# A list schedule that knows the array tile of each TensorE step and counts a change of tile

## The chip, the core and the metric

The kernel runs on one core of one Trainium2 chip. The core has TensorE (PE in the profile; its weight loads are PEld), VectorE (DVE), ScalarE (ACT), GpSimd (POOL) and SyncE (SP), which issues DMAs. Each engine executes its instructions in the order in which the program gives them and waits on semaphores for the others. The metric is the device time of one launch in microseconds (us). Three runs of the kernel before took 1405.84 to 1409.65 us, with a median of 1408.31 us.

## What is computed

One layer of a hybrid decoder: 16 meta tokens and 1024 tokens of width 1024, float32. Four mixers share one input projection, their outputs are concatenated and projected, and a mixture of 16 experts with two experts per token follows.

```python
h = layernorm(concat(meta, x))
ua, ub, uc, ud = split(h @ w_in)
ya = swa_attention(ua)          # window 128, 4 heads, softmax with sinks
yb = diff_attention(ub)         # two softmax maps per head, p0 - lam * p1
yc = rwkv7_mix(uc)              # the step below, token after token
yd = conv_module(ud)            # depthwise convolution of width 31, group norm, silu
h = layernorm(ALPHA * h + concat(ya, yb, yc, yd) @ w_out)
h = layernorm(ALPHA * h + moe(h))

def step(S, inp):               # rwkv7: 4 heads, state S of 64 x 64 per head
    r_t, w_t, k_t, v_t, kk_t, a_t = inp
    sa = einsum('bhij,bhj->bhi', S, -kk_t)
    S = S * w_t[:, :, None, :] + sa[..., None] * (kk_t * a_t)[:, :, None, :] + v_t[..., None] * k_t[:, :, None, :]
    return S, einsum('bhij,bhj->bhi', S, r_t)
```

## The kernel before

The program has three stretches. Stage 1 (up to about 206 us) normalizes the input and makes the projected columns of the RWKV mixer and of the convolution. Stage 2 makes the remaining projections, the convolution, both attentions and the RWKV mixer, and then the output projection with the routing. Stage 3 runs the experts. The change touches the order of stage 2 alone, up to the output projection.

**Stage 2's parts.** The projections (`project`, matmuls on L860) make ten column units, each from 72 matmuls: three column chunks (400, 384 and 256 wide), each in three steps of eight matmuls (high by high, high by low, low by high halves). Their results go out to DRAM and come back as the attention's operands once all of them are done (`switch`, then `load_qk` on L1302 and `values` on L1269). The convolution (`conv`) is 62 VectorE operations on 128 x 1024 (60 of them on L1184), followed by a group norm (`Norms`: a TensorE step on L1140, a subtraction, a square on ACT, a TensorE step on L1151, then logarithm and exponential on ACT). `swa` and `diff` are the attention blocks: scores (L1360, L1361, L1464), softmax, transposes (L1387, L1395, L1525), products with the values (L1407, L1408, L1539), and a last transpose of the outputs (L1585).

**The RWKV mixer** works on 17 chunks of 64 tokens in nine groups: the first has one chunk, the others two. `prep(i)` builds a group's matrices: gram matrices (L939), transposes (L966, L983), one product on L993, and then the inverse of a triangular matrix X in five levels. A level is a transpose on VectorE (L1010), a TensorE step (L993, `prep<-Tt,gs`), a masking on VectorE (L1017), a TensorE step (L993, `prep<-X,um`) and an addition on VectorE (L1024). A group's first X is made on GpSimd (L953, L954) and waits for the last X of the group before, so that the levels of all groups form one chain. `chain(i)` then takes the state through each chunk: L1056, a VectorE addition, L1079, copies on ACT and VectorE, L1095, VectorE for the new state (L1102), and L1118 and L1120 for the chunk's output. `rwkv_post` (norm, bonus, gate: L1140 to L1226) finishes each half of the sequence. The output projection (`out_block`, first matmul on L1823) needs all four mixers.

**What sets the order.** Each piece of work is a `Step` with an engine, a cost, dependencies and a priority. `Steps.run` simulates the engines and, again and again, takes the step that can start first; among steps that can start at the same time, the lower priority number wins. A step can start when its dependencies have ended (plus 0.2 where they ran on another engine), when its buffers are free and when its engine is free:

```python
t = max(t, free.get(s.eng, 0.0))
key = (t, s.prio, s.n)
```

The priorities of the projections are 20 to 29, of the attention blocks 10 to 57, of RWKV groups 0 to 3 just under 0, and of groups 4 to 8 between 10 and 55 (`PRG`). The code of the chosen step is written out at once, so the order of choice is the order on each engine.

**Tiles of the array.** Most TensorE steps use the whole array, 128 rows by 128 columns. The RWKV steps use part of it: 64 x 64 (L966, L993, L1056, L1079, L1118), 64 x 128 (L939, L983) or 128 x 64 (L1095, L1120). The profile prints this tile behind the names of a matmul (`128*128`, `64*64`).

## Time and profile before

| what | value |
|---|---|
| median of three runs | 1408.31 us (1405.84 to 1409.65) |
| the profiled execution's own time | 1411.35 us |
| its span, first to last instruction | 1409.5 us |
| mean granted TensorE clock, share of full speed | 0.927 |
| PE busy, share of the span | 1221.4 us, 87% |
| DVE / ACT / POOL busy | 908.9 / 627.2 / 278.5 us |
| stage 2 from the first projection to the first output projection matmul | 206.3 to 693.7 us |

A busy engine is one that has an instruction under way. On PE, consecutive matmuls overlap, and so the time that a matmul really takes from the engine is read from the distance between starts. A timeline row merges like instructions that follow one another; on PE one program matmul of float32 appears as two records in the rows of the RWKV steps.

### The profile page before, as it was taken

How to read it: one execution, taken by the hardware profiler on the slowest of the kernel's cores; microseconds unless marked ns; L12 is line 12 of the kernel's file. 1: busy time of each engine (PE TensorE's matmuls, PEld its weight loads, DVE VectorE, ACT ScalarE, POOL GpSimd, SP SyncE). 2: the span in 40 equal slices, each digit the busy share in tenths (PEclk: the TensorE clock that was granted, in tenths of full speed). 3: DMA queues.
4: the chain of work that ended last, by engine and by line, in shares of the span. 5: the costliest groups of instructions: out<-in, count | busy, mean ns of one | idle time of the engine just before them, and what ended most of it. 6: DMA issues, size and time to landing. Idle time of an engine off the chain costs nothing. (4 is left out here: it accounts for less than half of the span.)

```text
span 1409.5 us, 22368 instructions
## 1 busy us (share of the span) xinstructions
PE 1221.4 (87%) x8095; PEld 1006.0 (71%) x8095; DVE 908.9 (64%) x1682; ACT 627.2 (44%) x1109; POOL 278.5 (20%) x252
## 2 busy tenths in 40 slices
PE   5998899999979899789699948898989899889950
PEld 4886799887857788667477736776777777767840
DVE  7556739996235667477667785856457863866175
ACT  6453211233124655357733225656346653645151
POOL 3523203321111122133001121111111111121100
PEclk9999999999987999879899968998999999999985
DMA  8213245421180230501252547969887992996352
GB/s 205 84 47 111 103 132 183 140 86 56 54 213 20 55 88 11 113 24 57 85 179 91 179 151 232 357 191 302 239 240 233 326 341 65 333 317 196 97 181 120
DMA packets 165466, 219.65 MB, mean 156 GB/s; under 512 B 36047, under 2 KB 134491, under 8 KB 165037
## 3 DMA queue, kind: packets, MB, share of 16 engines
q1 hardware_dynamic: 156604, 188.66, 42.1%
q0 software_dynamic: 8688, 28.87, 8.6%
q8 instruction: 86, 1.41, 0.4%
q14 instruction: 88, 0.71, 0.2%
HBM read 174.38 MB, written 45.46 MB: 156 GB/s over the span
## 5 line engine op out<-in xcount | busy, mean ns | idle before, releaser
L454 PE MATMUL acc<-hh,wh 128*128 128x256 f32 (+2 forms) x288 | 96.8, 337 | 0.0
L454 PE MATMUL acc<-hh,wl 128*128 128x256 f32 (+2 forms) x288 | 93.3, 325 | 0.6 <-DVE wl L342 0.6
L1184 DVE SCALAR_TENSOR_TENSOR CY<-MX,cvw,CY 128x1024 f32<-128x1024 f32 x60 | 89.1, 1506 | 0.1
L2121 PE MATMUL rw<-wh,at 128*128 128x512 f32 x224 | 82.8, 420 | 7.2 <-ACT at L2096 3.1
L454 PE MATMUL acc<-hl,wh 128*128 128x256 f32 (+2 forms) x288 | 87.5, 322 | 0.0
L1665 DVE TENSOR_TENSOR wl<-MX,wh 128x1024 fp32r<-128x1024 f32 x66 | 78.2, 1219 | 6.8 <-ACT wh L1661 4.7
L2125 POOL DMA_INDIRECT acc__132<-y,ixs x21 | 40.8, 1945 | 181.5 <-issue 59.4
L1665 DVE TENSOR_TENSOR wol<-MX,woh 128x1024 fp32r<-128x1024 f32 x51 | 61.1, 1222 | 13.7 <-ACT woh L1661 12.5
L1661 ACT ACTIVATE wh<-MX 128x1024 fp32r<-128x1024 f32 x66 | 66.9, 1050 | 3.8 <-DMA MX<-in_exp_w_dram 2.2
L1482 ACT ACTIVATE E<-sc,nm 128x144 f32<-128x144 f32 (+7 forms) x64 | 48.0, 751 | 27.0 <-DVE nm L1476 22.6
L454 PEld LDWEIGHTS acc<-hh,wh 128*128 128x128 f32 x288 | 55.5, 193 | 5.7 <-issue 5.2
L1661 ACT ACTIVATE woh<-MX 128x1024 fp32r<-128x1024 f32 x51 | 52.1, 1051 | 13.5 <-DMA MX<-in_exp_w_dram 7.7
L2121 PEld LDWEIGHTS rw<-wh,at 128*128 128x128 f32 x224 | 43.7, 196 | 18.4 <-ACT at L2096 3.6
L454 PEld LDWEIGHTS acc<-hh,wl 128*128 128x128 f32 x288 | 55.3, 192 | 1.9 <-DVE wl L342 0.9
L1823 PE MATMUL oacc<-woh,mh 128*128 128x512 f32 x128 | 54.7, 428 | 1.7 <-ACT woh L1775 1.7
L2097 DVE TENSOR_TENSOR xte<-acc,xte 128x512 fp32r<-128x512 f32 x44 | 28.5, 684 | 38.8 <-ACT xte L2096 38.8
L454 PEld LDWEIGHTS acc<-hl,wh 128*128 128x128 f32 x288 | 53.3, 189 | 0.0
L1823 PE MATMUL oacc<-wol,mh 128*128 128x512 f32 x128 | 52.0, 406 | 1.5 <-DVE wol L1778 1.5
L1823 PE MATMUL oacc<-woh,ml 128*128 128x512 f32 x128 | 51.3, 401 | 0.0
L1506 POOL TENSOR_TENSOR E<-E,rho 128x272 f32<-128x272 f32 (+3 forms) x16 | 21.0, 1313 | 150.1 <-DVE rho L1500 71.2
L1539 PE MATMUL tp<-vs,at 128*128 128x128 f32 x352 | 48.8, 290 | 0.6 <-ACT at L1528 0.3
L2096 ACT ACTIVATE at<-tp 128x256 fp32r<-128x256 f32 x46 | 17.6, 382 | 70.8 <-PE tp L2094 56.4
(472 smaller groups left out, 3452.9 us busy)
## 6 DMA issues: line engine op xcount, KB each, us to landing
MX<-in_exp_w_dram SPq DMA_DIRECT2D x192, 256.0 KB
MX<-in_exp_w_dram SPq DMA_DIRECT2D x48, 512.0 KB
CY<-in_exp_w_dram SPq DMA_DIRECT2D x64, 256.0 KB
raw<-in_w_in_dram SPq DMA_DIRECT2D x20, 512.0 KB
qk<-dqk SPq DMA_DIRECT2D x64, 130.0 KB
CY<-in_exp_w_dram SPq DMA_DIRECT2D x16, 512.0 KB
dab<-ab SPq DMA_DIRECT2D x2, 2176.0 KB
qk<-dqk SPq DMA_DIRECT2D x16, 260.0 KB
```

Of the source, the lines that this page charges most:

```text
L454: T.matmul(v.acc[:, :wid], wt[:, k], x[:, k, c0:c0 + wid], start=(z + y == 0 and wt is w.h), stop=(z + y == len(ks) - 1))
L1184: V.scalar_tensor_tensor(y, hc[:, M + j:M + j + S], cvw[:, ct, j:j + 1], y, op0=ALU.mult, op1=ALU.add)
L1482: ACT.activation(w.E[:, c, off:W], w.sc[c][:, :W - off], AF.Exp, bias=w.nm[:, c:c + 1], scale=-1.0, accum_out=w.s[:, c:c + 1])
L1506: G.tensor_tensor(w.E[:, 1, :W], w.E[:, 1, :W], w.rho.to_broadcast([P, W]), op=ALU.mult)
L1539: T.matmul(o, w.at[:, j], vs[:, j, vc], start=(j == 0), stop=(j == blocks[-1]))
L1661: ACT.activation(slot_h[i % HLS][0], raw[i], AF.Copy)
L1665: eng.tensor_tensor(l, raw[i], h.bitcast(F32), op=ALU.subtract)
L1823: T.matmul(v.o, x_[:, k], y_[k][:, 512 * n:512 * n + 512], start=(i == 0 and j == 0), stop=False)
L2096: ACT.activation(dst[:, 0, s], tb[:, :m * P], AF.Copy)
L2097: V.tensor_tensor(dst[:, 1, s], tb[:, :m * P], dst[:, 0, s].bitcast(F32), op=ALU.subtract)
L2121: T.matmul(o[n], at[:, x, k * P:(k + 1) * P], w[k][y][:, n * 512:n * 512 + 512], start=(k == 0 and (x, y) == (0, 0)), stop=(k == 3 and x = ...
L2125: G.indirect_dma_start(out=acc_, out_offset=bass.IndirectOffsetOnAxis(ap=ix[:, 0:1], axis=0), in_=y, in_offset=None, compute_op=ALU.add)
```

## The change

Each TensorE step gets a `kind`, a pair of letters for its first and its last matmul's tile: `m` for the whole array (the default), `q` for 64 x 64, `r` for 64 x 128 and `c` for 128 x 64. The scheduler keeps the tile that the last TensorE step left behind. Where a step's first tile is another one, its earliest start on TensorE is counted 0.09 later. The step's cost is as before, no instruction's code is changed, and no priority.

```diff
-    LAT = LATN
+    LAT, CHANGE = LATN, 0.09
...
-    def add(self, eng, cost, fn, deps=(), prio=0.0, take=(), use=()):
+    def add(self, eng, cost, fn, deps=(), prio=0.0, take=(), use=(), kind=None):
+
         s = Step()
+        s.kind = kind or ("m", "m")
...
     def run(self):
-        free = {}
+        free, tile_ = {}, "m"
...
-                t = max(t, free.get(s.eng, 0.0))
+                t = max(t, free.get(s.eng, 0.0) + (self.CHANGE if s.eng == "PE" and s.kind[0] != tile_ else 0.0))
                 key = (t, s.prio, s.n)
...
             s.end = free[s.eng] = t + s.cost
+            if s.eng == "PE":
+                tile_ = s.kind[1]
             s.fn()
...
-        a = add("PE", .12 * n, vt1, [o.loaded], pr, take=[sv, o.sbz], use=[o.slot])
+        a = add("PE", .12 * n, vt1, [o.loaded], pr, take=[sv, o.sbz], use=[o.slot], kind="qq")
...
-            a = add("PE", .06 * n, b1, [vd], pr, take=[sb], use=[o.slot])
+            a = add("PE", .06 * n, b1, [vd], pr, take=[sb], use=[o.slot], kind="rr")
...
-                a = add("PE", .43, h1, sad, pr, take=[sh, ns], use=[o.sbz])
+                a = add("PE", .43, h1, sad, pr, take=[sh, ns], use=[o.sbz], kind="cc")
```

The other RWKV steps get their letters in the same way: `rr` for L939; `qq` for the steps on L993, L1056 and L1079; `cc` for the output of a chunk on L1118 and L1120.

The instructions of the projection stretch, the attention and the RWKV mixer come out in another order on every engine. Up to the first RWKV step of stage 2, and from the first matmul of the output projection on, TensorE's order is the same as before. In the changed kernel the line numbers are 4 or 5 higher.

**TensorE, where the first RWKV group began.** `acc` is a projection's accumulator, `wh` and `wl` its weights, `hh` and `hl` the input; `prep` is the RWKV preparation. Before:

```order
L860 MATMUL acc<-hh,wh_1755 128x384 x8
L860 MATMUL acc<-hh,wh_1755 128x256 x8
L860 MATMUL acc<-hl,wh_1755 128x384 x8
L939 MATMUL prep<-abv 128x128 x2
L860 MATMUL acc<-hh,wl_1756 128x384 x8
L939 MATMUL prep<-abv 128x128 x2
L860 MATMUL acc<-hl,wh_1755 128x256 x8
L860 MATMUL acc<-hh,wh_1866 128x400 x8
L966 MATMUL prep<-c__63,vch 64x64 x4
L860 MATMUL acc<-hh,wl_1756 128x256 x8
```

The same place in the changed kernel:

```order
L864 MATMUL acc<-hh,wh_1755 128x384 x8
L864 MATMUL acc<-hh,wh_1755 128x256 x8
L864 MATMUL acc<-hl,wh_1755 128x384 x8
L864 MATMUL acc<-hl,wh_1755 128x256 x8
L864 MATMUL acc<-hh,wl_1756 128x384 x8
L864 MATMUL acc<-hh,wl_1756 128x256 x8
L864 MATMUL acc<-hh,wh_1866 128x400 x8
L864 MATMUL acc<-hh,wh_1866 128x384 x8
```

The RWKV steps have left the projections: the first of them now stands behind the last projection matmul, and only the convolution's norm steps (L1145, L1156) stand between projections.

**TensorE, ahead of the output projection.** `E` holds softmax rows, `vs` and `at` values and transposed weights, `o` the attention's output, `chain` the RWKV chunks. Before:

```order
L1525 MATMUL tp<-c__63,E 128x128 x3
L1539 MATMUL tp<-vs,at 128x128 x6
L1525 MATMUL tp<-c__63,E 128x128 x4
L1539 MATMUL tp<-vs,at 128x128 x4
L1223 MATMUL tp<-xg,g2s 128x512 x2
L1585 MATMUL tp<-c__63,o 128x128 x4
L1823 MATMUL oacc<-woh_6941,mh_6953 128x512
```

The same place in the changed kernel; ahead of the first row stand eight more steps on L998 without another step between them, and behind the last one follow L1156, L1228 and the first output projection matmul (L1828):

```order
L998 MATMUL prep<-X,um 64x64 x8
L1084 MATMUL chain<-r,X 64x64 x4
L1100 MATMUL chain<-bz 64x64 x4
L1125 MATMUL chain<-gs,bz 64x64 x2
L1123 MATMUL chain<-abv,s_6744 64x64 x4
L1125 MATMUL chain<-gs,bz 64x64 x2
L1061 MATMUL chain<-s_6880,abv 64x64 x4
L1084 MATMUL chain<-r,X 64x64 x4
L1125 MATMUL chain<-gs,bz 64x64 x2
L1123 MATMUL chain<-abv,s_6880 64x64 x4
L1125 MATMUL chain<-gs,bz 64x64 x2
L1145 MATMUL tp<-MX,bdm 128x512 x2
```

What stood last before was the attention; what stands last now is the RWKV mixer's last two groups and its post-processing. Behind the last `tp<-vs,at` step there are 22 steps on L998 in the changed kernel (the two of each of ten levels, and one product for each of two groups) and none before.

## Rows read from the trace of the kernel before

**Rows 1.** Busy time by stretch (us from:to, length, engines with counts, PEclk, DMA, GB/s).

```profile
206.20:389.80 183.60, 179.81 (x1654) 154.94 (x1655) 132.41 (x188) 49.90 (x91) 46.96 (x34) 1.00 0.32 100
389.80:425.80 36.00, 25.44 (x316) 20.79 (x315) 10.63 (x31) 9.99 (x29) 3.13 (x6) 0.77 0.82 208
425.80:684.10 258.30, 231.12 (x2369) 193.64 (x2366) 171.93 (x545) 148.88 (x394) 62.49 (x60) 0.90 0.21 51
```

**Rows 2.** Timeline of TensorE in the projections (start, us, engine, line, names, tile, count).

```profile
212.06 3.01 PE L860 MATMUL acc<-hh,wl 128*128 128x400 f32 x16
214.91 2.55 PE L860 MATMUL acc<-hh,wh 128*128 128x256 f32 x16
217.30 2.56 PE L860 MATMUL acc<-hl,wh 128*128 128x256 f32 x16
...
222.09 2.50 PE L860 MATMUL acc<-hh,wh 128*128 128x384 f32 x16
224.42 1.57 PE L860 MATMUL acc<-hl,wh 128*128 128x384 f32 x8
...
348.70 2.66 PE L860 MATMUL acc<-hl,wh 128*128 128x256 f32 x16
351.29 0.68 PE L993 MATMUL prep<-Tt,gs 64*64 64x64 f32 x16
```

**Rows 3.** Groups of VectorE from 214.3 to 327.6 us (count, busy, mean ns, idle before).

```profile
L1184 DVE SCALAR_TENSOR_TENSOR CY<-MX,cvw,CY 128x1024 f32<-128x1024 f32 x55 | 83.1, 1526 | 0.1
L877 DVE SCALAR_TENSOR_TENSOR qlo<-acc,qhi 128x400 fp32r<-128x400 f32 (+2 forms) x18 | 9.0, 503 | 4.8 <-ACT qhi L873 4.8
```

**Rows 4.** The convolution's line: duration min/median/max in ns, first and last start.

```profile
L1184 DVE SCALAR_TENSOR_TENSOR CY<-MX,cvw,CY x60: 1232/1274/3250, 197.5 to 326.3; 128x1024 f32<-128x1024 f32 x60
```

**Rows 5.** Timeline of TensorE behind the projections: first value transposes, first differential scores.

```profile
405.27 1.94 PE L1282 MATMUL tp<-c__63,E 128*128 128x128 f32 x8 [5.40 <-DMA E<-dvv]
...
425.85 0.70 PE L1464 MATMUL sc<-qk,qk 128*128 128x144 f32 x2
```

**Rows 6.** Levels of the RWKV inverse: timeline of PE and DVE, clock of 423 to 426.

```profile
389.75 0.68 PE L993 MATMUL prep<-Tt,gs 64*64 64x64 f32 x16
390.95 0.68 PE L993 MATMUL prep<-X,um 64*64 64x64 f32 x16 [0.53 <-DVE um L1017]
391.68 0.42 DVE L1024 TENSOR_TENSOR X<-prep,X 128x256 f32<-128x256 f32 x1 [0.38 <-PE prep L993]
386.03 0.45 DVE L1010 STREAM_TRANSPOSE Tt<-X 128x256 f32<-128x256 f32 x1
...
423.00:426.00 3.00, 2.32 (x33) 2.02 (x33) 0.55 (x3) 0.00 (x0) 0.00 (x0) 0.50 0.00 0
423.15 1.12 PE L993 MATMUL prep<-Tt,gs 64*64 64x64 f32 x16 [0.78 <-DVE gs L942]
424.80 1.12 PE L993 MATMUL prep<-X,um 64*64 64x64 f32 x16 [0.53 <-DVE um L1017]
425.96 0.42 DVE L1024 TENSOR_TENSOR X<-prep,X 128x256 f32<-128x256 f32 x1 [1.22 <-PE prep L993]
```

**Rows 7.** Timeline: a group's first X, a conv norm, and stage 2's end.

```profile
310.16 2.52 POOL L953 TENSOR_TENSOR X<-gs,c 64x256 f32<-64x256 f32 x2
283.96 1.98 PE L1140 MATMUL tp<-CY,bdm 128*128 128x512 f32 x4
293.49 1.15 ACT L1168 ACTIVATE sq<-sq 128x512 f32<-128x512 f32 x2
...
662.75 0.34 PE L1120 MATMUL chain<-gs,bz 128*64 128x64 f32 x4
682.61 1.50 PE L1539 MATMUL tp<-vs,at 128*128 128x128 f32 x8
685.89 1.40 DVE L1226 SCALAR_TENSOR_TENSOR MX<-MX,lxb,tp 128x512 f32<-128x512 f32 x2
693.67 0.80 PE L1823 MATMUL oacc<-woh,mh 128*128 128x512 f32 x1 [1.72 <-ACT woh L1775]
```

More of the change, by code (lines that the diff above doesn't have):

```diff
@@ L942, in f2 @@
                 V.tensor_tensor(o.gs[:, par], small["pu"].rearrange("p (a c) -> p a c", c=P)[:, :n], b3(gmask, n), op=ALU.mult)
-            m = add("PE", .22 * n, f1, [o.loaded] + gfirst, pr, take=[sl] + ([] if gfirst else [o.sgs]), use=[o.slot] + ([o.sgs] if gfirst else []))
+            m = add("PE", .22 * n, f1, [o.loaded] + gfirst, pr, take=[sl] + ([] if gfirst else [o.sgs]), use=[o.slot] + ([o.sgs] if gfirst else []),
+                    kind="rr")
             gfirst = gfirst or [m]
@@ L1001, in lv2 @@
             ACT.activation(o.lv.rearrange("p a b c -> p (a b c)"), small["pu"][:, :n * C], AF.Copy)
-        a = add("PE", .12 * n, lv1, gdone + [vd], pr, take=[sl_, o.slv], use=[o.sgs, o.sbz])
+        a = add("PE", .12 * n, lv1, gdone + [vd], pr, take=[sl_, o.slv], use=[o.sgs, o.sbz], kind="qq")
         o.lvd = add("ACT", act(n * C), lv2, [a], pr, use=[sl_, o.slv])
@@ L1026, in prep @@
             a = add("DVE", dve(n * C), tr, [o.Xd], pr, take=[stt], use=[sX])
-            a = add("PE", .12 * n, u1, [a], pr, take=[su_, sum_], use=[stt, o.sgs])
+            a = add("PE", .12 * n, u1, [a], pr, take=[su_, sum_], use=[stt, o.sgs], kind="qq")
             a = add("DVE", dve(n * C), u2, [a], pr, use=[su_, sum_])
-            a = add("PE", .12 * n, x1, [a], pr, take=[sx_, sX1], use=[sum_, sX])
+            a = add("PE", .12 * n, x1, [a], pr, take=[sx_, sX1], use=[sum_, sX], kind="qq")
             o.Xd = add("DVE", dve(n * C), x2, [a], pr, use=[sx_, sX, sX1])
@@ L1064, in f3 @@
                         G.tensor_scalar(w.sp0[:, ct], w.s0[:, ct], pend[:, ct, c:c + 1], None, op0=ALU.mult)
-                a = add("PE", .25, f1, [sdone, o.loaded], pr, take=[ss_, sr], use=[sslot, o.slot])
+                a = add("PE", .25, f1, [sdone, o.loaded], pr, take=[ss_, sr], use=[sslot, o.slot], kind="qq")
                 rd = add("DVE", dve(P), f2, [a, o.lvd], pr, use=[ss_, sr, o.slv])
@@ L1085, in g3 @@
                 V.tensor_copy(o.bz[HALF[1], 1, 1, ci::o.nc], p2(small["cs"])[HALF[1]])
-            a = add("PE", .25, g1, [rd, o.Xd], pr, take=[scs], use=[sr, o.sX])
+            a = add("PE", .25, g1, [rd, o.Xd], pr, take=[scs], use=[sr, o.sX], kind="qq")
             sad = [add("ACT", act(P), g2, [a] + o.bzd, pr, use=[scs, o.sbz]), add("DVE", dve(P), g3, [a] + o.bzd, pr, use=[scs, o.sbz])]
@@ L1123, in y2 @@
                     ACT.activation(MX[:, 4:6, (c - 1) * C:c * C], p2(small["cy"]), AF.Copy)
-                a = add("PE", .7, y1, sad, pr + .05, take=[sy], use=[s0slot, o.slot, o.sbz, o.sgs])
+                a = add("PE", .7, y1, sad, pr + .05, take=[sy], use=[s0slot, o.slot, o.sbz, o.sgs], kind="cc")
                 ydone[c] = add("ACT", act(P), y2, [a], pr + .05, use=[sy])
```

## The prediction

> **What bounds the kernel now.** I read the stretches first, then TensorE's timeline in each, then the waits at their ends. From the first projection matmul to the last one, TensorE is busy in 179.8 of 183.6 us at full clock [rows 1]: it is the bound there, and what it does besides the 720 projection matmuls (RWKV groups 0 to 3, four norm steps, changes of tile) lengthens the stretch. VectorE is nearly as full, with the convolution until 327.6 us (its last tap starts at 326.3 and takes 1.27) [rows 4]. Then come 36 us in which TensorE is busy in 25.4 and the DMA engines in 82% of the time: the attention's operands come back from DRAM, and 5.40 us of that is a bare wait [rows 1, 5]. From 425.8 to 684.1 us attention and RWKV alternate; TensorE is busy in 231.1 of 258.3 us, so 27.2 us are idle. At 684.1 the last value product ends [rows 7], and 9.6 us later the output projection begins. Before the change, then, attention and RWKV end together.
>
> **What a change of tile costs.** Sixteen projection matmuls (eight of 256 and eight of 400 columns) take 217.30 - 214.91 = 2.39 us from start to start among their like, and 351.29 - 348.70 = 2.59 us with an RWKV step of another tile on either side [rows 2]. That is 0.10 us a side; the RWKV step pays something too. So the 0.09 that the scheduler now counts is the right size. Counting the changes in the two orders gives 356 before and 258 now in stage 2: 98 fewer, which is 98 x 0.10 = 10 us of TensorE's time.
>
> **What the change moves.** The saving is small beside the new order. The projections are always ready and of the default tile; an RWKV step is of another tile and so counts as startable 0.09 later; and the start time is compared ahead of the priority. So whole-array steps win over RWKV steps for as long as one is ready, whatever the priorities say, and RWKV goes to where nothing else can start. By the order, nothing of RWKV stands among the projections any more, and the work is pushed back towards the end. With it go its issues on the queues: on SP most of the group loads now stand behind the loads of the attention's operands, and nothing but the pushed-back RWKV work waits for them; on POOL the first X of each group leaves the neighbourhood of the projections' weight splits, for which only the convolution's taps could be glad (their median is 1.27 us, the longest 3.25 [rows 4]); I count nothing for it. I cost four terms.
>
> First, the projections. A unit's nine steps are three of each width; the neighbours 400 and 384 take 214.91 - 212.06 = 2.85 us, 256 and 400 take 2.39, 384 and 256 take 224.42 - 222.09 = 2.33 [rows 2]. Half of the three is 3.79, times three is 11.4 us a unit, and ten units are 114 us. The four norm steps add 8 us (two take 1.98 us [rows 7], and there are four pairs). TensorE alone would end at 206.3 + 122 = 328 us. But VectorE now is the late one: from 214.3 us it still has 55 taps of 83.1 us in all and 20 evacuations of 0.50 us [rows 3], which end at 307.5 us, and some 5 us of the first half's norm and activation lie among them. The second half's norm step needs the last tap, and 152 projection matmuls stand behind it: 152/720 x 114 = 24 us, and some 2 us for the norm's second step. I take 337 us against 389.8: **-53 us**, with bounds of -62 (VectorE hidden) and -48.
>
> Second, the wait for the operands, 36 us before. The same transfers follow the same last projection, and DMA sets their pace [rows 1]; RWKV work fills less of it now, which nobody waits for. **0 us**, bounds -5 and +5.
>
> Third, the attention stretch. Between the first differential scores and the last value product the order now holds 17 more RWKV steps on L993 and 13 more on the other RWKV lines. At 0.68 us each [rows 2] that is 20 us, if all of it lies on the path. Some falls into the stretch's 27.2 us of idle time [rows 1]. I take **+12 us**, bounds -6 (idle time takes all of it, and whole-array steps run in longer rows) and +25 (each extra step is also a place where TensorE, in order, waits for VectorE).
>
> Fourth, the end. Behind the last value product now stands the serial part of two groups: ten levels, a first X, the last two chunks, the post-processing. At full clock a level goes from its first TensorE step to its second in 390.95 - 389.75 = 1.20 us, from there to the addition in 391.68 - 390.95 = 0.73, and needs 0.42 for the addition and 0.45 for the transpose: 2.80 us. At 423 us, with the granted clock at 0.50 (the lower level, 1.2 GHz), it is 1.65 + 1.16 + 0.42 + 0.45 = 3.68 us [rows 6]. TensorE is idle for more than half of such a level, and it was so ahead of 423 us too; I take 3.3 us, 33 us for ten (28 to 37). The first X has three GpSimd operations, two of which take 2.52 us [rows 7]: 3.8 us. The last two chunks are five hops between TensorE and its readers at 1.20 to 1.65 us each, and about 1 us for the last outputs: 7 to 9 us. The norm takes 294.6 - 284.0 = 10.7 us in the convolution's case, with taps in between; with bonus and gate I take 14. Before, from the last chunk's output to the end of the gate, it was 687.29 - 662.75 = 24.5 us with attention in between, which is the upper bound. From the gate to the first output matmul it is 693.67 - 687.29 = 6.4 us, with the same splits. Sum: 33 + 3.8 + 7.2 + 14 + 6.4 = 64 us against 9.6 before: **+54 us**, bounds +45 and +70. Attention no longer covers this chain, and the output projection's weights load under it.
>
> The Trainium skill, page "TensorE: Matmul & The Clock Gate", part 1 (the HAM clock gate), says that a gate passes fewer clock pulses to an array that has been idle; by that rule all ten levels would run at the lower level, 36.8 us and not 33, and the sum would be 4 us higher; the 0.50 at 423 us behind gaps agrees [rows 6].
>
> Behind the first output matmul each engine has the same work in the same order, so I carry the shift through to the end. The sum is -53 + 0 + 12 + 54 = **+13 us**. On the profiled execution's own 1411.35 us that gives 1424; the median of the runs is 3.0 us lower, so I predict **1422 us**.
>
> **The rivals.** *Faster: the attention stretch soaks up the pushed-back work.* The sign hangs on the third term: with the others as above the sum is zero where the stretch shrinks by 1 us. If its idle time takes the extra steps and fewer interruptions shorten it by 6 us, and the end is at its lower bound, the sum is -53 - 6 + 45 = -14 us: 1394 us. For it speak 27 us of idle time and the mean clock of 0.90 there [rows 1], which has room to rise; against it, that 30 more steps are interleaved in order, and that the 22 steps behind the attention are there in any case. The Trainium skill, page "TensorEngine Tiling (Array Packing)", section "Tiling Modes", states that a change of tiling mode drains TensorE; by it alone, fewer changes mean a shorter run, 10 us less, and the trace shows that cost. That result needs the end to be hidden, so it belongs to this rival.
>
> *Much slower: the pushed-back chain stalls TensorE in order.* If each of the extra steps in the attention costs its upper bound (+25), VectorE holds the projections (-48) and the end runs at the lower clock throughout (+65), the sum is +42: 1450 us. For it speaks that RWKV steps are what TensorE waited at in the attention stretch, as at 390.95 us [rows 6]; against it, that the scheduler placed them where it thought them ready.
>
> *Nothing to measure.* Terms one and four cancel within 2 us (-53 and +54); if the third is hidden in idle time altogether, the sum is +1 us and the time 1409 us. The change not doing what it says is no rival: the order shows the regrouping.
>
> **How the numbers follow.** A measurement of this kernel can tell about 0.3% (4 us) from no change. I give the forecast (1414 to 1438 us) 0.50, the faster rival 0.20, the much slower one 0.15, and the one in between 0.15; these add to chances of 0.20 for faster, 0.13 for within 0.3%, and 0.67 for slower, since a little of the last one reaches above the bound. The range of 8 in 10 reaches to 1396, a little above the faster rival's time, and to 1446, short of the much slower one's.
>
> **What would show it right or wrong.** In the changed kernel's profile the projection line should run in one block from 206 us and end near 337 us, with TensorE waiting for the convolution near its norm steps. The first differential scores should start near 373 us, and the last value product end near 643. Then some 64 us should follow in which TensorE alternates with VectorE on the level lines, mostly idle and at the lower clock, and the first output projection matmul should start near 707 us. The prediction is wrong if the last value product ends before 630 us or after 665, or if the levels behind it take less than 2.5 us each. If the projections end near 328, VectorE was not late; if the output projection starts before 693.7 us, the faster rival has won.

## The result and the profile after

The changed kernel takes 1449.55 us (median of six runs, 1444.2 to 1453.66), the kernel before 1409.26 us in the runs beside it (1405.84 to 1416.4). The ratio is 1.0272, 95% interval 1.0242 to 1.0303: slower by 40 us, where 1422 us (+13) was forecast and the range ended at 1446. The profiled execution took 1448.16 us, with a span of 1446.4 and a mean granted clock of 0.902 (0.927 before).

The stretches of the changed kernel, cut at the events of [rows 1], with the end as a stretch of its own (us from:to, length, then busy time and count of PE, PEld, DVE, ACT and POOL, the granted clock, DMA share, GB/s):

```profile
205.70:337.70 132.00, 122.86 (x736) 117.17 (x736) 101.96 (x101) 40.45 (x61) 27.07 (x11) 0.97 0.38 122
337.70:372.50 34.80, 22.69 (x230) 17.68 (x229) 9.85 (x33) 10.52 (x30) 4.10 (x8) 0.75 0.79 195
372.50:646.80 274.30, 249.15 (x2741) 213.30 (x2742) 181.67 (x571) 144.31 (x392) 70.08 (x71) 0.88 0.21 50
646.80:736.50 89.70, 56.86 (x640) 42.46 (x640) 31.34 (x79) 20.49 (x42) 6.08 (x15) 0.58 0.09 32
```

The first cut here is the start of the last projection matmul (337.68 us), 0.3 us ahead of its end (337.96), where [rows 1] are cut. The table goes by the end.

| term | before, us | after, us | difference | forecast (bounds) |
|---|---|---|---|---|
| projections | 183.6 | 132.2 | -51 | -53 (-62 to -48) |
| wait for the operands | 36.0 | 34.5 | -1 | 0 (-5 to +5) |
| attention stretch | 258.3 | 274.3 | +16 | +12 (-6 to +25) |
| last value product to first output matmul | 9.6 | 89.7 | +80 | +54 (+45 to +70) |

Three terms are where they were put, and the fourth is 26 us larger than its estimate and 10 us beyond its bound. That term is the miss. From the first output matmul (736.54 us) to the end the profiled execution of after is 6 us shorter than that of before, with the same instructions in the same order. This is no part of the change: from the last output matmul to the end, the fifteen profiled executions of this study took 581 to 597 us. Stretches are therefore compared below, and total times through the medians.

**The end, read closely.** TensorE in the changed kernel around the last value product and in the first level behind it (timeline: start, us, engine, line, names, tile, count, idle before with its releaser; line numbers are 4 or 5 higher than before). L1100 and L1061 are steps of chunks 11 and 12, L998 is the level, L943 the last group's gram; the VectorE row is the transpose that the level needs.

```profile
646.08 0.71 PE L1544 MATMUL tp<-vs,at 128*128 128x128 f32 x4
649.02 0.45 DVE L1015 STREAM_TRANSPOSE Tt<-X 128x256 f32<-128x256 f32 x1
649.04 0.45 PE L1100 MATMUL chain<-bz 128*64 128x64 f32 x8 [0.67 <-DVE bz L1090]
650.84 0.69 PE L1061 MATMUL chain<-s,abv 64*64 64x64 f32 x8 [0.58 <-DVE s L1107]
...
656.53 0.69 PE L1061 MATMUL chain<-s,abv 64*64 64x64 f32 x8 [0.68 <-DVE s L1107]
657.01 1.06 PE L998 MATMUL prep<-Tt,gs 64*64 64x64 f32 x16
...
660.69 2.07 PE L943 MATMUL prep<-abv 64*128 64x128 f32 x8 [0.53 <-DVE X L1029]
662.80 0.69 DVE L946 TENSOR_TENSOR gs<-prep,c 128x512 f32<-128x512 f32 x1 [1.69 <-PE prep L943]
663.55 1.12 PE L998 MATMUL prep<-Tt,gs 64*64 64x64 f32 x16 [0.79 <-DVE gs L946]
```

The level's transpose is done at 649.5 us, but its TensorE step starts at 657.01: TensorE works in order, and the steps of chunks 11 and 12 stand ahead. Five of them (three shown) carry the state on, and these wait for readers on VectorE or ScalarE. Then, between the first level and the second, the last group's gram takes 2.07 us on TensorE and 0.69 on VectorE, in the one `prep` buffer that the level also uses: 663.55 - 657.01 = 6.54 us for a level. The next ones start at 669.70, 675.49 and 680.01.

The end of the next to last group's levels, then the lone levels of the last group, and the clock there (the last two rows are busy times as above):

```profile
683.37 0.37 PE L1084 MATMUL chain<-r,X 64*64 64x64 f32 x2 [0.53 <-DVE X L1029]
...
699.14 1.12 PE L998 MATMUL prep<-Tt,gs 64*64 64x64 f32 x16 [1.01 <-DVE Tt L1015]
700.79 1.12 PE L998 MATMUL prep<-X,um 64*64 64x64 f32 x16 [0.53 <-DVE um L1022]
...
702.91 1.12 PE L998 MATMUL prep<-Tt,gs 64*64 64x64 f32 x16 [1.01 <-DVE Tt L1015]
...
710.07 0.69 PE L1084 MATMUL chain<-r,X 64*64 64x64 f32 x8 [0.62 <-DVE X L1029]
718.71 3.63 PE L1145 MATMUL tp<-MX,bdm 128*128 128x512 f32 x4 [0.38 <-ACT MX L1128]
736.54 0.79 PE L1828 MATMUL oacc<-woh,mh 128*128 128x512 f32 x1 [8.77 <-ACT woh L1780]
...
660.00:680.00 20.00, 13.31 (x136) 11.05 (x132) 6.14 (x13) 1.14 (x3) 0.98 (x2) 0.50 0.00 1
700.00:710.00 10.00, 5.86 (x86) 4.73 (x82) 3.44 (x8) 0.00 (x0) 0.00 (x0) 0.50 0.00 0
```

A lone level takes 702.91 - 699.14 = 3.77 us at a granted clock of 0.50, the lower level; its two TensorE steps are 1.12 us each, as they were at 423 us before and not the 0.68 of the higher level [rows 6]. From the last chunks' first step to the norm it is 8.6 us, from there to the output projection 17.8. So the end is 10 us ahead of the first level, 26 us for the next to last group's five levels (657.01 to 683.37), 27 us for the last group's (with chunks 13 and 14 ahead of and inside the first of them), 9 for the last two chunks and 18 behind.

### The profile page after: what moved, and what is told of

Its sections match the earlier page's. It is cut to its first block, busy times and chain, and to the rows that moved or that the text cites. A ratio compares the mean times of both kernels' runs of the same rounds, so it can differ in the third digit from the quotient of the medians.

```text
span 1446.4 us, 22361 instructions
## 1 busy us (share of the span) xinstructions
PE 1225.6 (85%) x8095; PEld 1020.4 (71%) x8095; DVE 910.6 (63%) x1682; ACT 625.9 (43%) x1107; POOL 268.5 (19%) x252
## 5 line engine op out<-in xcount | busy, mean ns | idle before, releaser
L1670 DVE TENSOR_TENSOR wol<-MX,woh 128x1024 fp32r<-128x1024 f32 x51 | 61.0, 1221 | 16.5 <-ACT woh L1666 10.6
L1828 PE MATMUL oacc<-woh,mh 128*128 128x512 f32 x128 | 54.8, 428 | 8.8 <-ACT woh L1780 8.8
L1828 PE MATMUL oacc<-wol,mh 128*128 128x512 f32 x128 | 51.7, 404 | 1.7 <-DVE wol L1783 1.6
L1828 PE MATMUL oacc<-woh,ml 128*128 128x512 f32 x128 | 51.3, 401 | 0.0
L2102 DVE TENSOR_TENSOR at<-tp,at 128x256 fp32r<-128x256 f32 x46 | 19.3, 419 | 48.2 <-ACT at L2101 44.8
L998 PE MATMUL prep<-Tt,gs 64*64 64x64 f32 x680 | 38.8, 272 | 11.7 <-DVE Tt L1015 4.0
L2101 ACT ACTIVATE xte<-acc 128x512 fp32r<-128x512 f32 x44 | 24.0, 596 | 54.6 <-PE acc L2099 24.5
```

The costliest lines, as they stand in the source:

```text
L998: T.matmul(dst[q, j * C:(j + 1) * C], lhs(q, r, j, par), rhs(q, r, j, par), start=True, stop=True)
L1670: eng.tensor_tensor(l, raw[i], h.bitcast(F32), op=ALU.subtract)
L1828: T.matmul(v.o, x_[:, k], y_[k][:, 512 * n:512 * n + 512], start=(i == 0 and j == 0), stop=False)
L2101: ACT.activation(dst[:, 0, s], tb[:, :m * P], AF.Copy)
L2102: V.tensor_tensor(dst[:, 1, s], tb[:, :m * P], dst[:, 0, s].bitcast(F32), op=ALU.subtract)
```

## The experiments

My theory before them: counting the way into RWKV's tiles ranks every ready whole-array step ahead of RWKV, RWKV's chain is pushed behind the attention, and there it is slow for three reasons (chunk steps ahead in order, the last group's preparation in between, the lower clock). The rivals: the size of the count, the knowledge of the time itself, the order within the attention, or something else that holds the output projection back.

### The size of the count

```diff
-    LAT, CHANGE = LATN, 0.09
+    LAT, CHANGE = LATN, 0.001
```

> The changed kernel with the counted change of tile at 0.001 instead of 0.09. Theory (the count is a rank: any amount above zero puts a ready whole-array step ahead of a ready RWKV step, before the priorities are asked): the projections again run in one block and end near 338 us, the last value product ends near 645, some 85 us of RWKV and post-processing stand behind it, time 1438 to 1456 us. Rival (the amount matters: 0.09 is too much and a small one leaves the priorities in force): projections end near 390, nothing of RWKV behind the last value product, 1403 to 1415 us.

Measured: 1439.43 us, ratio 1.0214 (1.0175 to 1.0253). The projections end at 339.0 us, the last value product at 633.6 (expected near 645), and 87.7 us lie behind it. Its attention stretch, columns as above:

```profile
374.10:633.60 259.50, 241.15 (x2759) 204.41 (x2760) 179.79 (x571) 143.36 (x394) 67.06 (x70) 0.92 0.22 53
```

A count of a ninetieth does nearly the same: it is a rank and not a cost. What it doesn't do is the 16 us in the attention. With as many RWKV instructions there, this order needs 259.5 us and not 274.3, at a clock of 0.92 instead of 0.88. Why this order keeps the higher clock I did not settle; one place where they differ is the gram, ahead of which TensorE idles 5.9 us in the changed kernel's attention stretch and 1.2 us here (groups of TensorE in the two stretches, last figure idle before):

```profile
L943 PE MATMUL prep<-abv 64*128 64x128 f32 x96 | 16.6, 323 | 5.9 <-DVE X L1029 5.9
...
L943 PE MATMUL prep<-abv 64*128 64x128 f32 x96 | 14.8, 298 | 1.2 <-DVE X L1029 1.2
```

### The knowledge without the choice

```diff
-                t = max(t, free.get(s.eng, 0.0) + (self.CHANGE if s.eng == "PE" and s.kind[0] != tile_ else 0.0))
+                t = max(t, free.get(s.eng, 0.0))
...
-            s.end = free[s.eng] = t + s.cost
+            s.end = free[s.eng] = t + s.cost + (self.CHANGE if s.eng == "PE" and s.kind[0] != tile_ else 0.0)
```

> The changed kernel with the 0.09 added to the step's end and not to its start: the schedule knows the time of a change of tile, but does not choose by it. Theory (the loss comes from the choice, not from the knowledge of the time): the order is nearly that of before (145 of TensorE's rows still lie among the projections, none of RWKV behind the last value product), projections end 385 to 395 us, first output matmul 688 to 700, time 1402 to 1416 us. Rival (a schedule with longer RWKV steps pushes them back by itself): over 1425 us.

Measured: 1427.88 us, ratio 1.0135 (1.0097 to 1.0172). The theory missed by 12 us, and the time is the one that the rival named (over 1425). The rival's reason is not what happened, since nothing of RWKV stands behind the last value product and the first output matmul follows 12.2 us later. But the projections took 188.1 us (183.3 before, cut in the same way) and the attention 269.1, so that the first output matmul came at 709.7 us and not by 700:

```profile
205.50:393.60 188.10, 181.30 (x1660) 155.88 (x1660) 131.91 (x189) 49.84 (x90) 45.08 (x36) 1.00 0.31 97
428.40:697.50 269.10, 233.38 (x2350) 193.67 (x2349) 174.03 (x539) 150.80 (x393) 62.71 (x60) 0.89 0.20 49
```

TensorE is busy 233.4 us there, 2 us more than before, so the rest is idle time: 35.7 us against 27.2. The level's second step shows about half of it. The group of this step in the attention stretch of before, and then of this kernel:

```profile
L993 PE MATMUL prep<-X,um 64*64 64x64 f32 x356 | 16.7, 237 | 8.3 <-DVE um L1017 8.1
...
L998 PE MATMUL prep<-X,um 64*64 64x64 f32 x352 | 16.3, 237 | 13.0 <-DVE um L1022 13.0
```

TensorE waits for the masking there for 13.0 us in all, against 8.3. A schedule that is told of longer steps was no better by that alone. Why just this order waits more, and why its projections are longer, I did not settle; with the tiny count above it says that an order's details move the attention by some 10 us either way.

### One way only

Counting only the way out of RWKV's tiles:

```diff
-                t = max(t, free.get(s.eng, 0.0) + (self.CHANGE if s.eng == "PE" and s.kind[0] != tile_ else 0.0))
+                t = max(t, free.get(s.eng, 0.0) + (self.CHANGE if s.eng == "PE" and s.kind[0] != tile_ and s.kind[0] == "m" else 0.0))
```

and only the way in:

```diff
-                t = max(t, free.get(s.eng, 0.0) + (self.CHANGE if s.eng == "PE" and s.kind[0] != tile_ else 0.0))
+                t = max(t, free.get(s.eng, 0.0) + (self.CHANGE if s.eng == "PE" and s.kind[0] != tile_ and tile_ == "m" else 0.0))
```

> The changed kernel, the change counted only where a whole-array step would follow an RWKV step: another RWKV step of any tile is then preferred, and a whole-array step is never preferred over a ready RWKV step. Theory (the loss comes from counting the way into RWKV's tiles): nothing stands behind the last value product, 8 changes of tile fewer than before (348 against 356), which at 0.10 us is under 1 us: 1400 to 1414 us, within 0.5% of before. Rival (any preference among tiles costs): over 1420 us.

> The mirror of the kernel with only the way out counted: 0.09 only where an RWKV step would follow a whole-array step. Theory (the way in is what pushes RWKV back): no RWKV among the projections, they end near 338 us, 80 to 95 us stand behind the last value product, 1435 to 1455 us. Rival (it takes both ways): within 1% of before, 1400 to 1424 us.

Measured: way out 1415.36 us, ratio 1.0045 (1.0018 to 1.0072), a microsecond above the expected interval; way in 1457.79 us, ratio 1.0336 (1.0296 to 1.0375), 3 us above its expected interval and by the medians 8 us slower than the changed kernel itself, though the two intervals of the ratio just overlap. The attention with the way out, then the end with the way in:

```profile
426.50:685.20 258.70, 226.70 (x2322) 190.62 (x2318) 172.93 (x543) 148.56 (x392) 61.13 (x60) 0.91 0.21 51
...
654.50:744.20 89.70, 57.06 (x641) 42.37 (x640) 31.38 (x79) 20.55 (x42) 6.11 (x15) 0.57 0.09 32
```

With the way out the first output matmul starts at 694.0 us, as before; with the way in, the end is 89.7 us, as in the changed kernel. The way in is what displaces RWKV.

### Is the end really RWKV's chain?

Levels two to five of the last two groups issue nothing, in the changed kernel and in the kernel before:

```diff
         for li in range(5):
+            gone = i >= len(GR) - 2 and li > 0
...
+            if gone:
+                tr = u1 = u2 = x1 = x2 = lambda: None
             a = add("DVE", dve(n * C), tr, [o.Xd], pr, take=[stt], use=[sX])
```

> The changed kernel without levels two to five of the last two RWKV groups (their steps stay in the schedule and issue nothing; these two groups' inverses are left incomplete). Theory (the end behind the last value product is this chain, uncovered: levels of 4.5 to 6.2 us in the one group and 3.77 in the other): the end shrinks from 90 to 52 to 64 us and the time falls to 1412 to 1425 us; it stays above 64 where the second group's preparation, and not the first group's levels, sets the pace. Rival (something else holds the output projection back, its weights or GpSimd's queue): the end stays at 85 us or more and the time at 1443 or above.

> The kernel before without levels two to five of the last two RWKV groups (their steps stay in the schedule and issue nothing; these inverses are left incomplete). Theory (in the kernel before these levels lie beside the attention and only their instructions on TensorE and VectorE cost anything): 8 levels of two TensorE steps at 0.68 us and the changes of tile with them can give at most some 11 us, and waits for them a little: 1394 to 1408 us, so at most half of the 24 us that the same cut gave in the changed kernel. Rival (the chain is the bound in the kernel before, too): 1380 to 1388 us.

Measured: from after 1425.24 us, ratio to before 1.0100 (1.0062 to 1.0138), which is 24 us less than the changed kernel; from before 1406.06 us, ratio 0.9963 (0.9941 to 0.9986), 4 us less. The end of the first, then the attention of the second:

```profile
643.90:703.30 59.40, 37.77 (x386) 26.41 (x385) 21.08 (x56) 20.59 (x42) 6.08 (x15) 0.64 0.14 47
...
423.10:677.30 254.20, 221.74 (x2111) 185.27 (x2110) 164.01 (x521) 148.65 (x394) 62.38 (x60) 0.89 0.21 51
```

The same eight levels are worth 89.7 - 59.4 = 30 us in the end of the changed kernel and 4 us in the attention of the kernel before. In the end these levels lie open, and in the kernel before the attention had covered them.

### The three parts of the excess

First, no TensorE instructions of chunks 11 to 14:

```diff
+            four_ = [] if c in (11, 12, 13, 14) else four
...
-                def f1(w=w, ci=ci, four=four):
+                def f1(w=w, ci=ci, four=four_):
```

(and the same for `g1`, `h1` and `y1`).

> The changed kernel without the TensorE instructions of chunks 11 to 14 (their readers on the other engines stay; the state is left wrong). Theory (in TensorE's order these steps stand ahead of and between the levels of the last two groups, and each waits for its own chain of readers): the next to last group's first level starts within 3 us of the last value product instead of 10, the levels between the chunk steps close up, and the end is 72 to 79 us instead of 90; time 1432 to 1440 us. Rival (the chunk steps only fill time in which the levels wait for VectorE): the end is 86 us or more.

Measured: 1443.06 us, ratio 1.0216 (1.0176 to 1.0257), 3 us above the expected interval; an end of 80.9 us, 8.8 less, which misses its interval by 2 us. The first level starts 5.7 us behind the last value product (648.2), not within 3 (the last two rows are the start and the end of the last group's part):

```profile
649.28 0.46 PE L988 MATMUL prep<-c__63,abv 64*128 64x64 f32 x4 [0.48 <-ACT lv L1006]
...
653.88 1.12 PE L998 MATMUL prep<-Tt,gs 64*64 64x64 f32 x16 [2.04 <-ACT bz L991]
...
680.31 1.12 PE L998 MATMUL prep<-bz,gs 64*64 64x64 f32 x16 [0.53 <-DVE X L1029]
...
702.44 0.69 PE L1085 MATMUL chain<-r,X 64*64 64x64 f32 x8 [0.62 <-DVE X L1029]
```

The group's own transposes (L988) hold the buffer next, and ScalarE empties it late, behind the attention's last normalization. So the chunk steps were part of that wait, and ScalarE's queue was right behind them. Of the 8.8 us only 4.5 are saved here. The next to last group's levels take 26.4 us as in the changed kernel, and some 4.6 us are saved in the last group's part, 702.44 - 680.31 = 22.1 us instead of 710.07 - 683.37 = 26.7, where chunks 13 and 14 had stood ahead of and inside the first level.

Second, no gram and transposes of the last group:

```diff
+        cts = range(0 if i == len(GR) - 1 else 2)
...
-                for ct in range(2):
+                for ct in cts:
                     for ci in range(nc_):
                         j = idx(ct, ci)
                         T.matmul(small["pu"][:, j * P:(j + 1) * P], fl(o.ab[q, ct, ci, 2:4]), fl(o.ab[q, ct, ci, 0:2]), start=True, stop=True)
```

(and the same at the transposes).

> The changed kernel without the gram and transpose matmuls of the last RWKV group (their readers on the other engines stay; this group's matrices are left wrong). Theory (these steps lie between the levels of the group ahead and share the one prep buffer with them): that group's levels shrink from 4.5 to 6.2 us to 3.7 to 4.8, five of them by some 5 us, and the end is 82 to 87 us instead of 90; more does not go, since the reads of the buffer on VectorE and ScalarE stay. Rival (the levels are long because of the clock alone): they stay over 4.5 us and the end at 88 or more.

Measured: 1443.31 us, ratio 1.0222 (1.0191 to 1.0253); an end of 83.0 us, 6.7 less. The next to last group's levels start at 658.60 us and then at

```profile
663.18 0.68 PE L999 MATMUL prep<-Tt,gs 64*64 64x64 f32 x16 [1.58 <-DVE gs L947]
666.86 1.12 PE L999 MATMUL prep<-Tt,gs 64*64 64x64 f32 x16 [1.57 <-DVE gs L947]
671.01 1.12 PE L999 MATMUL prep<-Tt,gs 64*64 64x64 f32 x16 [1.39 <-ACT bz L977]
674.94 1.12 PE L999 MATMUL prep<-Tt,gs 64*64 64x64 f32 x16 [1.10 <-DVE Tt L1016]
```

that is 3.7 to 4.6 us each, where the changed kernel needed 4.5 to 6.5. The last group's preparation was a real price. How much of it is the shared buffer and how much the time of its matmuls on TensorE is not shown: the readers that empty the buffer stay here, and the levels still wait for them (`gs` at L947).

Third, the clock. Idle matmuls fill TensorE's pauses in the levels. In the first version they write to columns of the `prep` buffer that nobody reads:

```diff
                 mm(small["pu"], lambda q, r, j, par: o.gs[q, par, j, 0:C], lambda q, r, j, par: w.Tt[q, j])
+                if i >= len(GR) - 2:
+                    T.matmul(small["pu"][:, 256:512], bdm, fl(o.X), start=True, stop=True)
...
                 mm(small["pu"], lambda q, r, j, par: w.um[q, j], lambda q, r, j, par: o.X[q, j])
+                for _ in range(2 if i >= len(GR) - 2 else 0):
+                    T.matmul(small["pu"][:, 256:512], bdm, fl(o.X), start=True, stop=True)
```

> The changed kernel with idle matmuls in the levels of the last two RWKV groups: one of 128 x 256 behind a level's first TensorE step, two behind its second, into a part of the prep buffer that nobody reads. Theory (the lone levels take 3.77 us because TensorE's clock stands at 0.50 there): the granted clock of the end rises to 0.9 or more and a lone level takes 2.8 to 3.4 us although it now has more to do; the end is 84 to 92 us instead of 90. Rival (the level is set by VectorE and the hops between the engines, the clock matters little, or the clock stays at 0.50): a lone level takes 4.3 us or more, the end 95 to 105.

Measured: 1459.87 us, ratio 1.0345 (1.0309 to 1.0381); an end of 100.8 us, as the rival said, but not for its reason. A lone level of this kernel, and the clock around it:

```profile
705.71 0.68 PE L998 MATMUL prep<-Tt,gs 64*64 64x64 f32 x16 [0.99 <-DVE Tt L1015]
706.32 0.70 PE L1021 MATMUL prep<-X,bdm 128*128 128x256 f32 x2
707.06 0.42 DVE L1024 TENSOR_TENSOR um<-prep,c 128x256 f32<-128x256 f32 x1 [1.40 <-PE prep L1021]
...
701.00:721.00 20.00, 14.02 (x160) 9.57 (x160) 5.40 (x14) 0.28 (x1) 0.85 (x2) 0.90 0.01 2
```

The clock rose and the steps fell to 0.68 us. But VectorE's masking waits for the idle matmul (L1021), which writes to the same buffer, and so the filling lay on the path: 4.57 us a level. The second version writes to a part of the `chain` buffer that the levels don't touch, in the last group's last four levels alone:

```diff
+                for _ in range(2 if i == len(GR) - 1 and li else 0):
+                    T.matmul(small["cy"], bdm, bdm, start=True, stop=True)
```

(behind the level's first step, and four behind its second).

> The changed kernel with idle matmuls in the last group's last four levels, this time into a tile that no reader of a level waits for: two of 128 x 128 behind a level's first TensorE step, four behind its second. Theory (at the higher clock a level's two TensorE steps take 0.68 instead of 1.12 us each, and nothing else of it depends on the clock): the granted clock in these levels rises to 0.9 or more, a lone level takes 2.9 to 3.2 us instead of 3.77, the last two chunks 7 to 7.6 instead of 8.3, and the end is 84 to 88 us. Rival (the filling costs as much as the clock gives, or the clock stays at 0.50): a lone level takes 3.7 us or more, the end 89 to 95.

```profile
701.91 0.68 PE L998 MATMUL prep<-Tt,gs 64*64 64x64 f32 x16
702.52 0.71 PE L1021 MATMUL chain<-bdm 128*128 128x128 f32 x4
702.63 0.42 DVE L1024 TENSOR_TENSOR um<-prep,c 128x256 f32<-128x256 f32 x1 [0.80 <-PE prep L998]
...
704.86 0.68 PE L998 MATMUL prep<-Tt,gs 64*64 64x64 f32 x16
...
680.00:692.00 12.00, 9.28 (x132) 7.44 (x128) 3.46 (x11) 1.58 (x5) 1.46 (x4) 0.50 0.01 1
692.00:708.00 16.00, 14.97 (x206) 13.07 (x208) 5.90 (x14) 0.28 (x1) 0.72 (x2) 0.81 0.01 2
```

Now the masking starts beside the filling. The granted clock is 1.00 from 698 to 710 us, so three of the four filled levels have it; the first still has steps of 1.12 us. A lone level takes 704.86 - 701.91 = 2.95 us instead of 3.77, the last two chunks 7.4 instead of 8.6, and the end 85.2 us, 4.5 less. The median over six runs, 1449.17 us, ratio 1.0291 (1.0261 to 1.0322), shows no gain over the changed kernel; 4.5 us is about the width of these intervals, so the gain is shown for the stretch and not for the whole.

Last, the three cuts together:

> The three cuts of the end together, on the changed kernel: no TensorE instructions of chunks 11 to 14, none of the last group's gram and transposes, and the idle matmuls in the lone levels. Alone they took 8.8, 6.7 and 4.5 us off the end of 89.7 us. Theory (they are three parts of the end's excess, one after the other): the end is 67 to 73 us, within 9 us of the 64 that was forecast for it. Rival (they cover the same waits): 76 us or more.

Measured: 1432.62 us, ratio 1.0152 (1.0110 to 1.0194); its end:

```profile
646.10:718.00 71.90, 43.45 (x497) 32.16 (x496) 30.81 (x79) 20.05 (x42) 6.08 (x15) 0.69 0.12 39
```

71.9 us: 17.8 less than 89.7, where the three alone gave 8.8 + 6.7 + 4.5 = 20.0. They are separate parts for the most part. Some 7.5 us of the 25.3 over the forecast's 64.4 remain; ScalarE's late copies ahead of the first level, as above, and that only three of ten levels have the higher clock are what I see there, unmeasured each by itself.

### A version that helps

Counting after the projections only, so that RWKV keeps its places among them. In the first version the way in is not counted for the last group, in the second for none of the last five:

```diff
+        left = sum(s.kind == "pp" for s in self.todo)
...
+(self.CHANGE if s.eng == "PE" and not left and s.kind[0] != tile_ and (s.kind[0] == "m" or s.prio < 54) else 0.0))
...
+                left -= s.kind == "pp"
```

(`pp` is the kind of the projection steps; the second version has `s.prio < 0`.)

> The changed kernel, the change counted only once all projection steps are placed, and there both ways, except the way into the last RWKV group's chunk steps and levels. 333 changes of tile against 356 before, the projections as before. Theory (the loss is RWKV work displaced from the projections; in the attention alone the count only regroups): projections end near 390, the attention stretch takes 250 to 262 us, the last RWKV step moves up to the last value product, so that 15 to 24 us stand behind it instead of 9.6: 1406 to 1420 us. Rival (counting in the attention is itself the loss): over 1430 us.

> As the kernel before it, but in the attention the way in is not counted for any of the last five groups, only the way out. 339 changes of tile against 356 before, RWKV ends well ahead of the last value product. Theory: 17 changes fewer at 0.10 to 0.20 us give 2 to 3 us, within what an order moves by chance: 1400 to 1412 us, no version that beats the kernel before clearly. Rival (changes of tile in the attention are worth more than the rows show): under 1398 us.

Measured: 1407.53 us, ratio 0.9970 (0.9947 to 0.9993), and 1402.94 us, ratio 0.9955 (0.9929 to 0.9980). Attention and end of the first, then of the second:

```profile
421.40:673.40 252.00, 225.16 (x2367) 192.93 (x2366) 169.42 (x540) 140.40 (x384) 61.56 (x60) 0.89 0.20 46
673.40:691.80 18.40, 8.44 (x17) 2.52 (x15) 11.60 (x26) 14.31 (x22) 0.50 (x4) 0.71 0.35 122
...
421.10:678.30 257.20, 225.16 (x2334) 189.70 (x2334) 171.32 (x541) 151.16 (x396) 61.35 (x59) 0.92 0.22 51
678.30:687.40 9.10, 2.75 (x9) 0.95 (x7) 5.87 (x18) 6.20 (x10) 0.50 (x4) 0.88 0.19 72
```

Both are a little faster than the kernel before. The first gains 3.8 us ahead of the attention and 6.3 in it, and gives 8.8 back in its end, where the last chunk comes too late. The second keeps RWKV ahead of the end and gains 4.7 us between the start of the last projection matmul and the first differential scores (421.1 - 389.5 = 31.6 against 425.8 - 389.5 = 36.3). The forecast for it, no clear gain, was too careful by little: 8 us in the median, 6 by the ratio, with the interval under 1. That the counted change of tile is the reason is not shown: the gain of the second lies mainly ahead of the attention, and other orders moved by more than this without it being meant.

## Why the prediction was right in its sign and wrong in its size

**First term (-53, measured -51): right, and for the reason given.** The projections ran in one block to 338.0 us (337 forecast). TensorE alone would have needed less. It waited 6.48 us for the last tap of the convolution's first half, 1.76 us for the last of the second half, and 9.1 us in all (timeline of TensorE there, and the busy times of three microseconds):

```profile
289.08 3.41 PE L1145 MATMUL tp<-CY,bdm 128*128 128x512 f32 x4 [6.48 <-DVE CY L1189]
291.87 2.02 PE L864 MATMUL acc<-hh,wl 128*128 128x384 f32 x8
...
310.61 1.96 PE L1145 MATMUL tp<-CY,bdm 128*128 128x512 f32 x4 [1.76 <-DVE CY L1189]
...
289.00:292.00 3.00, 2.92 (x5) 1.36 (x5) 2.96 (x4) 0.00 (x0) 0.00 (x0) 0.50 0.33 113
```

The second and the last row show a cost that I had not counted: behind the first wait the granted clock was at its lower level, 0.50 from 289 to 292 us, and eight matmuls begun there took 2.02 us instead of 1.55. The last tap started at 309.2 us, and with it VectorE set the end as in the sum; 152 projection matmuls stood behind it, as counted.

**Second term (0, measured -1): right.** The length hardly changed, though less RWKV work lay in it (183 of its matmul records instead of 270).

**Third term (+12, measured +16): the size was right, the working only partly.** By the distances between starts on TensorE, the RWKV rows of the stretch take 94.6 us after and 67.6 before, 27 more and not 20; all other rows take 154.6 instead of 163.5, 9 less; idle time is 25 us instead of 27. The sum is 16. The 9 us are not the saved changes of tile. By the two orders, the attention stretch has 196 changes after and 188 before; the saving lies among the projections, with 1 after and 143 before, and 37 changes more stand in the end. Among the projections the whole-array rows take 123.0 us instead of 133.5, 10.5 less or 0.07 a change. That is near the 10 us of the prediction, and the first term's 114 us already held it. The Trainium skill's drain at a change of mode (page "TensorEngine Tiling (Array Packing)", section "Tiling Modes") agrees with these 10.5 us. Of the 9 us some 3 are norm steps of RWKV's post-processing that now lie in the end. Where the rest comes from is not settled; fewer interruptions alone don't explain it, since the kernel with the tiny count goes between RWKV and the other rows 177 times there (160 before, 145 after) and its other rows take 154.8 us as well. The kernel with the tiny count did nearly the same work in 259.5 us: its RWKV rows take 86.1 us, with a higher clock, and it idles 18 us. The term depends on the order by 15 us, and that my +12 was near is partly luck.

**Fourth term (+54, measured +80): the step that failed.** The mechanism was named (levels, first X, chunks, norm and gate, uncovered), and it is what happened. Its price was taken from lone levels one after the other, with nothing ahead of or between them, and these were not alone:

- Ahead of the first level I counted nothing. It took 10.2 us. The chunk steps of the group before stood ahead in TensorE's order. They were in the order that I had; I took only the last two chunks into the sum. Without the TensorE instructions of four chunks it takes 5.7 us, and there the level waits for ScalarE to empty the buffer.
- The five levels of the next to last group were taken at 3.3 us, 16.5 in all, and took 26.4. The last group's gram and transposes lie between them, in a single buffer. Without these the end is 6.7 us shorter. The first X, which I added at 3.8 us, in turn took nothing on top: it lay beside the next to last group's last level.
- The five levels of the last group, also 16.5 us in the sum, took 26.7. Chunks 13 and 14 stood ahead of and inside the first of them; without their TensorE instructions it is 22.1 us.
- The lower clock held from 660 to 720 us. The 3.3 us were between 2.80 and 3.68; the lone levels took 3.77. The sentence with the Trainium skill, page "TensorE: Matmul & The Clock Gate", part 1, that all levels would run at the lower level, agrees with the 0.50 in every stretch from 660 to 720 us, and the filled kernel shows the other side: more work on TensorE, and 2.95 us a level. That would have been +4 of the 26, and it is part of the levels' times above.
- Norm, bonus and gate (13.9 us for 14) and the last two chunks (8.3 to their last output, for 7.2) were about right; the first output matmul came 4.3 us later instead of 6.4. From the last chunks' first step on it is 26.5 us where 27.6 were counted.

In the sum of 64.4 us the differences are +10.2, +9.9 (next to last group), -3.8 (first X), +10.2 (last group) and -1.1, together 25.4, which makes up the measured 89.7 us but for rounding.

**The rivals.** *Much slower* named the right side, and its 1450 us is what was measured, but by another sum: +25 in the attention and +65 at the end, where it was +16 and +80. *Faster* fell with its condition that the end is hidden, and *nothing to measure* with its condition that terms one and four cancel: they were -51 and +80. What I called wrong if it happened (last value product before 630 or after 665, levels under 2.5 us) did not happen: it ended at 646.8 against 643, and no level took less than 3.3 us. The first output matmul, expected near 707, came at 736.5.

## What to carry to other kernels

A cost that a greedy list scheduler adds to a step's start is a rank, not a cost: here 0.001 displaced nearly the same work as 0.09, since the start is compared ahead of the priority. Ask of any such term which class of steps it can starve, and where that work goes when nothing covers it; counted only where it can't displace the serial chain, the kernel was not slower and perhaps a little faster. And when a chain is priced at the end of a stretch, read everything that stands between its steps in each engine's order, with the buffers they share: a lone step's time at the same clock was a lower bound here (3.77 us a level, 4.5 to 6.5 with other steps between).

## What the runs showed of the hardware that was not expected

Through a chain of small matmuls with pauses the granted clock of TensorE stayed at 0.50 for some 60 us (660 to 720). Filling the pauses with matmuls that nobody reads brought the clock up and a level from 3.77 to 2.95 us, where the filling wrote to a buffer that no reader on the path waits for; where it wrote to the level's own buffer, the level took 4.57. A change of tile next to projection matmuls shows in whole stretches too: 133.5 us of whole-array rows with 143 changes, 123.0 us with one. The last stretch of the kernel, the same instructions in the same order in every version, took 581 to 597 us, a spread that is larger than most of the effects measured here.
